# Exponentials of the decay sums loaded as rows, and several products, squares and loads moved, in a one-core decoder layer

## The chip, the cores and the metric

The kernel runs on one core of a Trainium2 chip. A core has five engines that run their own instruction streams side by side: PE (TensorE, matrix products), DVE (VectorE), ACT (ScalarE), POOL (GpSimd) and SP (SyncE), which here only issues loads; stores are issued by ACT. Data comes and goes through 16 DMA engines that all queues share. Each engine takes its instructions in order, and an instruction that waits holds up those behind it. The metric is device time in microseconds (us) from start to end of one execution.

## The reference

One layer of a decoder: the normed and modulated input h goes through one wide product into a gated spatial branch and a Mamba-2 branch, which are merged, projected and added to x.

```python
mod = silu(c) @ ada_w + ada_b                       # shift, scale, gate
h = rms_norm(x, norm_w) * (1 + scale) + shift       # x: 1024 x 1024
proj = h @ w_in                                     # 1024 x 11296
y_a = spatial_gating(gelu(gm_u), gelu(gm_v), ...) * silu(gm_z)
xbc = silu(causal_depthwise_conv(xbc, conv_w, conv_b)); xs, bm, cm = split(xbc)
dt = softplus(dt_raw + dt_bias); a = -exp(a_log)
y_b = ssd_scan(xs, dt, a, bm, cm) + xs * d_skip     # 8 groups, 32 heads of 64, state 128
y_b = rms_norm per group of (y_b * silu(ssm_z)), times ssm_norm_w
merged = sigmoid(g_a) * (y_a @ w_proj_a) + sigmoid(g_b) * (y_b @ w_proj_b)
out = rms_norm(x + gate * (merged @ w_out), final_norm_w)
```

The scan works in chunks of 128 rows. With A the running sum of dt * a inside a chunk, a chunk's output is

```python
y_diag = (C B^T * exp(A_l - A_s) for s <= l) @ (x dt)   # inside the chunk
y_off  = (C @ previous state) * exp(A_l)                # from the chunks before
state  = state * exp(A_end) + B^T @ (exp(A_end - A_s) * x dt)
```

The exp(A_l) of y_off, per head and row, is what the tile `ea` holds.

## The kernel before

**Stages.** In the profiled execution: up to 73 us the prologue (norm, modulation, the first gate product); to 149 us a block for the gated branch (V block); to 914 us the wide product as pairs of blocks with seven products in place of eight (`pair`, `jobs`), with convolutions, gates and the decay sums done beside it; to 1153 us the state-space stage; to 1340 us the product with `w_proj_b` (units p1, p3, p6, p5, p7, p2, p4 with eight parts each); then the output product. float32 operands are split into a high and a low part for the fast product format, so each product takes three matmuls (high x high, low x high, high x low).

**What sets the order.** Loads go through `load` (L90) on SP and keep the order of the program, as matmuls do (`mm` L81, `tp` L84). Stores go through `store` (L93) on ACT. `later(n, f)` puts a piece of work n slots on; a slot is one call of `run_tasks`. Other work on DVE, ACT and POOL is ordered by a scheduler, except where `pin` holds it in program order.

**Prologue.** For each of eight blocks, modulation rows (`pm`) are worked out and become `md` (DVE L275, L276), from which ACT and DVE form the operands of the gate product `acc`. SP loads `aw` and `w0r` for each block; between two of them the vectors `dtb`, `abc`, `dsk` (dt_bias, a_log, d_skip, each spread over 128 partitions). `small_parameters2` copies `dsk` into `dskt` on DVE (L503). The first product that uses `dskt` comes in the state-space stage.

**Decay sums.** `dt_part3`, about 745 us, holds A for 32 heads x 1024 rows in `act` and stores it as `acs_d`, one row of 4 heads x 256 per group and step.

**State-space stage.** 8 groups x 4 steps of 256 rows make 32 steps, two groups in turn. For each step n:
- `fetch` (SP): `dcy`, the row of `acs_d` spread over 128 partitions (512 KB), then `sl` (768 KB: C, B, x and silu(z) of the group). There are five sets of these tiles.
- `decay`: ACT takes the exponential of A for `ea` in two instructions of 64x512 (L1101), POOL masks `dcy` in place (L1104), ACT takes eight exponentials of it (L1109).
- `prep`: PE products `pc` and transposes `px`; DVE `xd`, `xe` (L1125), `dcy` times C B^T (L1129); ACT `bn` (L1131).
- `front`: PE `yi` and the state's product `sp`; the new state `st` on POOL (L1157) and DVE (L1159).
- `back`: PE `yn`; then `evacuate`: DVE `y` (L1185) and `ym` = yn * ea (L1189), POOL `y` + `ym` (L1190) and the gate product `yz` (L1191), which reads the last part of `sl` and so frees its buffer.
- after each second step `post`: two stores of `yz` to `yb_d` on ACT, then 5 slots on the squares (`squares`, in place in yz, ACT L1210 and POOL L1211), 17 slots on the row sums (`post2`: PE `pq`, DVE `ssq` L1221, POOL L1225). For the last half of the last two groups the squares go at once into other tiles (L1205, L1206), and the sums come after the loop.

`yz` has four buffers. Between these pieces, `draw` takes matmuls of the product with `w_proj_a` (`proj_a`, PE `pma`), 2 at a time, to fill PE. Its weights are cast to a high part (`wah`, ACT L1316) and a low part (`wal`, DVE L1317) one block of 128 columns ahead, after the second of eight products of the block before.

**Transition.** When the steps are done, all but five draws are taken, then `post2` of the last two groups, then `loads(u)` for the first six units of p1 (SP: `rb`, the row scales; `yn`, read from `yb_d`; `p1a`, `p1r`) with `operands` two units behind (DVE `yn` norm L1530; ACT `p1bh` L1567 and `p1a` L1572; their low parts on DVE), then the last draws, then `multiply` (L1592).

Of the kernel before, what the change touches and what calls it, by code (L numbers as in the profile page):

```python
# [8 lines left out]
F32 = mybir.dt.float32  # L9
# [26 lines left out]
def hybrid_kernel(  # L36
# [16 lines left out]
    def dt_(shape, name):  # L53
        return dram.tile(shape, F32, name=name, tag=name)

    acs_d = dt_([NG, 4, HPG, 256], "acs_d")
    rs_d = [dt_([1, S], f"rs_d{g}") for g in range(NG)]
    v_d = dt_([NG, P, NCH * P], "v_d")
    ya_d = [dt_([P, S], f"ya_d{g}") for g in range(NG)]
# [29 lines left out]
    def load(dst, src):  # L89
        pin(nc.sync.dma_start(dst, src))  # L90
# [77 lines left out]
    def wide(name, dt=F32):  # L168
        return w4[0].tile([P, S], dt, name=name, tag="w4", bufs=w4[1])


    with tc.tile_pool(name="p0", bufs=1, reuse_waits="tile") as p0:
# [278 lines left out]
        for n in range(1, KT):  # L451
            todo = prepare(n + 1) if n + 1 < KT else {}
            for at, _ in enumerate(first_products(n), 1):
                if at == 1 and n + 2 < KT:
                    load_aw(n + 2)
                    load_w0(n + 2)
                if at == 1 and n == 1:
                    load(dtb, dt_bias.to_broadcast([P, NH]))
                    load(abc, a_log.to_broadcast([P, NH]))
                    load(dsk, d_skip.to_broadcast([P, NH]))  # L460
                if at in todo:
                    todo[at]()
                if at == 2 and n < KT - 1:
                    split_w0(n + 1)
                between(n, at)
# [17 lines left out]

    def small_parameters():

        pkb = wide("pkb").rearrange("p (i q) -> p i q", q=P)
        G.memset(pkb[:, 0], 0.0)
        at = 0
        for src, n in [(conv_b, 32), (ssm_norm_w, 16), (gm_ln_w, 8), (gm_ln_b, 8)]:
            load(pkb[at : at + n, 0], src[0].rearrange("(r q) -> r q", q=P))  # L490
            at += n
        load(pkb[:, 1], conv_w[0].rearrange("k (i q) -> (k i) q", q=P))
        later(4, small_parameters2, pkb)
# [213 lines left out]
    def dt_part3():  # L707
        act = wide("act")[0:NH, :]
        for q in range(2):
            pt = bank(f"pact{q}")  # L710
            for i in range(4):
                ch = q * 4 + i
                tp(pt[0:NH, i * P : (i + 1) * P], nacs[:, ch * NH : (ch + 1) * NH], ident)
            V.tensor_scalar_mul(act[:, q * 512 : (q + 1) * 512], pt[0:NH, :], -1.0)
        for g in range(NG):
            store(acs_d[g].rearrange("s h t -> h s t"),
                  act[HPG * g : HPG * (g + 1), :].rearrange("h (s t) -> h s t", s=4))

    def mix_weights():

# [353 lines left out]
    class Group:  # L1074
# [5 lines left out]
        def fetch(self, s):  # L1080
            g, nm = self.g, f"{self.g}_{s}"
            n = nstep[0] % NSET
            nstep[0] += 1
            pool, b = (p2r, 2) if n < 2 else (p2q, NSET - 2)
            dcy = pool.tile([P, HPG, 2, P], F32, name=f"dcy{nm}", tag="dcy", bufs=b)
            load(dcy.rearrange("p h i l -> p (h i l)"),
                 acs_d[g, s].rearrange("h t -> (h t)").unsqueeze(0).to_broadcast([P, HPG * 256]))
            sl = pool.tile([P, 6, 256], F32, name=f"sl{nm}", tag="sl", bufs=b)
            load(sl, s_d[g][:, s])
            if n < 2:  # L1090
                ea = p2r.tile([P, 2, 256], F32, name=f"ea{nm}", tag="ea", bufs=2)
            else:
                ea = turn(ea_r, f"ea{nm}", F32).rearrange("p (j t) -> p j t", j=2)
            self.pre[s] = (sl, dcy, ea)

        def decay(self, s):

            g = self.g
            sl, dcy, ea = self.pre[s]
            for hh in range(2):  # L1100
                A.activation(ea[hh * HD : (hh + 1) * HD],  # L1101
                             dcy.rearrange("p (j e) i l -> p e j (i l)", e=2)[hh * HD : (hh + 1) * HD, hh], AF.Exp)
            d8 = dcy.rearrange("p h i l -> p (h i) l")
            G.affine_select(out=d8, in_=d8, compare_op=ALU.is_ge, fill=-1e30, base=0,  # L1104
                            pattern=[[0, 2 * HPG], [1, P]], channel_multiplier=-1)
            sub = fac(nacs, g, s)
            for i in range(2):
                for h in range(HPG):
                    A.activation(dcy[:, h, i, :], dcy[:, h, i, :], AF.Exp, bias=sub[:, i, h : h + 1])  # L1109
# [83 lines left out]
        def post(self, q):  # L1193

            g = self.g
            for j in range(2):
                store(yb_d[2 * g + j][:, q * 512 : (q + 1) * 512], self.yz[q][:, j])
            yz = self.yz[q]
            if g < NG - 2 or q == 0:
                later(5, self.squares, yz, [yz[:, j] for j in range(2)])  # L1200
                later(17, self.post2, q, [yz[:, 0]])
            else:
                self.late = sq = [turn(r, f"sq{g}", F32) for r in (ea_r, (ym_r, y1_r)[g % 2])]
                for j in range(2):
                    pin(A.activation(sq[j], yz[:, j], AF.Square))  # L1205
                G.tensor_add(sq[0], sq[0], sq[1])  # L1206

        def squares(self, yz, sq):
            for j in range(2):
# [102 lines left out]
    def wa_block(dd):  # L1312
        was[dd] = []
        for i, wr in enumerate(war.pop(dd)):
            wh, wl = turn(wah_r[0], f"wah{dd}_{i}"), turn(wal_r[0], f"wal{dd}_{i}")
            A.copy(wh, wr)  # L1316
            V.tensor_sub(wl, wr, f32(wh))  # L1317
            was[dd].append((wh, wl))

    def beside(n):  # L1320

        if n == 0:
            ya_load(0)
            ya_load(1)
        elif n == 1:
            for r, c in ((war_r, 2), (wah_r, 2), (wal_r, 2)):
                r.append(ring(c))
            wa_load(0)
            more = [room.pop(0) for _ in range(2)]
            room.extend(more)  # L1330
        elif n < 5:
            ya_load(2 * n - 2)
            ya_load(2 * n - 1)
        if n == 4:
            for k in range(2):
                ya_operand(k)
            wa_block(0)
            for k in range(2, 6):
                ya_operand(k)

# [56 lines left out]
    def proj_a():  # L1397

        for dd in range(KT):
            if dd + 2 < KT:  # L1400
                wa_load(dd + 2)
            ths, pms = [], []
            for h in range(2):
                th = turn(tha_r, f"tha{dd}_{h}", F32)
                load(th, th_d[dd * P : (dd + 1) * P, h * 512 : (h + 1) * 512])
                ths.append(th)
                pms.append(bank(f"pma{dd}_{h}"))
            for k in range(KT):
                wh, wl = was[dd][k // 4]
                yh, yl = yas[k]  # L1410
                ks = slice(k % 4 * P, (k % 4 + 1) * P)
                for n, (lw, r) in enumerate(((wh, yh), (wh, yl), (wl, yh))):
                    for h in range(2):
                        mm(pms[h], lw[:, ks], r[h], k + n == 0, k == KT - 1 and n == 2)
                    yield
                if k == 1 and dd + 1 < KT:
                    wa_block(dd + 1)
            keep = pin if dd == KT - 1 else lambda i: i
            for h in range(2):
                keep(V.scalar_tensor_tensor(ths[h], ths[h], 1.0, pms[h], op0=ALU.add, op1=ALU.mult))  # L1420
            for h in range(2):
                keep(nc.scalar.dma_start(mt_d[dd][:, h * 512 : (h + 1) * 512], ths[h]))
# [51 lines left out]
        run_tasks()  # L1474


    draw(left[0] - 5)
    for late in groups[NG - 2 :]:
        late.post2(1, late.late[:1])
    room.extend(ea_r[0] + [st_r[0][1]])  # L1480
    room.extend(tag for k in range(KT - 2) for tag in ya_tags[k])

# [200 lines left out]
    def ahead(u):  # L1683
        if u + LOAD < len(units):
            loads(u + LOAD)
        if u + LEAD < len(units):
            operands(u + LEAD)

    for u in range(LOAD):
        loads(u)  # L1690
        if u > 1:
            operands(u - 2)
    draw(left[0] + 1)
    room.extend(tag for k in (KT - 2, KT - 1) for tag in ya_tags[k])
    for tags, _ in (war_r[0], wah_r[0], wal_r[0], tha_r):
# [10 lines left out]
    for u, (nm, k) in enumerate(units):  # L1706
        if k == 0:
            if nm == "p1":
                first = {t: psb.tile([P, 512], F32, name=f"{t}p", tag=f"b{t}") for t in ('y0', 'y2', 'x0', 'x1', 'y1', 'x2', 'y3', 'x3')}
                psx, psy = ([first[f"{v}{j}"] for j in range(4)] for v in "xy")  # L1710
                rows_bank[0] = lambda name: psy[2 + ("pr6", "pr7").index(name)]
            elif nm in ("p5", "p2"):
                psy = banks(f"y{nm}", "y")
            ps = psy if nm in ("p2", "p5", "p3") else psx
# [216 lines left out]
```

## Time and profile before

| | us |
|---|---|
| median of three runs | 1400.12 |
| lowest, highest | 1399.70, 1400.92 |
| the profiled execution, its own time | 1404.41 |
| its span, first to last instruction | 1402.7 |
| mean granted PE clock of the profiled execution | 0.993 |

The profile is one execution. Times in it are counted from its first instruction. "Busy" is the time in which an engine executes; matmuls overlap each other a little, so the starts of matmuls, not their lengths, give their pace. A row of the timeline has start, length, engine, line, the tiles out<-in, and in brackets the idle time before it and what ended that. In the chain of waits each row is start, length, and what the end of the execution hung on at that moment. The granted clock is the share of full speed at which PE was let run.

### The profile page before, as it was taken

The page shows a single profiled execution, that of the slowest core. Times are in us where ns is not written, and L with a number is a line of the kernel's source. Part 1 is how long each engine was busy: PE and PEld are TensorE (multiplying, and loading weights), DVE is VectorE, ACT ScalarE, POOL GpSimd, SP SyncE. Part 2 cuts the span into 40 slices and gives each one's busy share as a digit, 9 for nine tenths or more (in the row PEclk, how much of TensorE's full clock was granted, in tenths as well). Part 3 has the DMA queues.
Part 4 walks back from the last instruction along what each step waited for, and adds up shares of the span by engine and source line. Part 5 has one row for each costly group of instructions (what it writes and reads, how often), then busy time and mean ns, then how long its engine had stood idle before and what let it go on. Part 6 is the DMA issues. An engine that isn't in the chain of part 4 may idle for free.

```text
span 1402.7 us, 20203 instructions
## 1 busy us (share of the span) xinstructions
PE 1370.8 (98%) x6951; PEld 1133.6 (81%) x6951; DVE 1041.7 (74%) x1724; ACT 800.0 (57%) x1447; POOL 189.1 (13%) x191
## 2 busy tenths in 40 slices
PE   8999999999999999999999999999999999999997
PEld 6588888888888888888888888888888877788786
DVE  4685876777778789788888885398777736859976
ACT  4664666667556566465576555677666714233443
POOL 1000000000000000000000000038868760000002
PEclk9999999999999999999999999999999999999999
DMA  8674534343435667787675764698787719978913
GB/s 265 176 234 137 151 120 121 100 126 118 130 99 148 195 196 246 229 260 210 196 218 177 234 205 139 212 362 305 270 272 266 266 65 323 346 250 298 381 63 120
DMA packets 247228, 288.60 MB, mean 206 GB/s; under 512 B 14509, under 2 KB 194133, under 8 KB 247125
## 3 DMA queue, kind: packets, MB, share of 16 engines
q1 hardware_dynamic: 173716, 203.76, 45.5%
q10 hardware_dynamic: 73408, 83.54, 17.5%
q8 instruction: 55, 0.90, 0.3%
q14 instruction: 49, 0.39, 0.1%
HBM read 199.79 MB, written 87.46 MB: 205 GB/s over the span
## 4 chain that ended last, share of the span: by engine, by line
PE 69%; DMA 11%; DVE 8%; ACT 4%; issue 3%; SPq 2%; POOL 2%; ACTq 0%; DVEq 0%; POOLq 0%
PE xz L565 6%; PE xx L565 6%; PE xg L565 5%; PE xcb L565 5%; PE xuz L565 5%; PE pma L81 3%; PE vx L954 3%; PE yx L565 3%; PE yz L565 3%; PE ycb L565 3%; PE yg L565 3%; PE ox L1775 2%; PE yuz L565 2%; SPq L90 2%; DMA yn<-yb_d 2%
## 5 line engine op out<-in xcount | busy, mean ns | idle before, releaser
L1104 POOL TENSOR_SCALAR_AFFINE_SELECT dcy<-dcy 128x1024 f32<-128x1024 f32 x32 | 35.0, 1092 | 794.6 <-DMA yl<-ya_d 748.6
L1109 ACT ACTIVATE dcy<-dcy,nacs 128x128 f32<-128x128 f32 x256 | 78.5, 388 | 14.1 <-POOL dcy L1104 13.7
L1101 ACT ACTIVATE ea<-dcy 64x512 f32<-64x512 f32 x64 | 40.1, 626 | 13.0 <-DMA dcy<-acs_d 12.5
L1189 DVE TENSOR_TENSOR ym<-yn,ea 128x512 f32<-128x512 f32 (+1 forms) x32 | 19.9, 622 | 32.8 <-PE yn L81 32.8
L81 PE MATMUL pma<-yh,wah 128*128 128x512 f32 x128 | 43.9, 424 | 0.0
L1129 DVE TENSOR_TENSOR dcy<-dcy,pc 128x1024 f32<-128x1024 f32 x32 | 38.9, 1217 | 5.0 <-PE pc L84 4.0
L81 PE MATMUL pma<-yh,wal 128*128 128x512 f32 x128 | 42.6, 414 | 0.0
L1024 ACT ACTIVATE ac<-ac 128x1024 f32<-128x1024 f32 x32 | 34.0, 1061 | 13.5 <-DVE ac L1022 13.2
L1191 POOL TENSOR_TENSOR yz<-y,sl 128x512 f32<-128x512 f32 x32 | 41.4, 1293 | 0.9
L81 PE MATMUL pma<-yl,wah 128*128 128x512 f32 x128 | 40.3, 396 | 0.0
L1530 DVE SCALAR_TENSOR_TENSOR yn<-yn,par,rb 128x512 f32<-128x512 f32 x32 | 23.8, 747 | 21.7 <-DMA yn<-yb_d 21.7
L1190 POOL TENSOR_TENSOR y<-y,ym 128x512 f32<-128x512 f32 (+1 forms) x32 | 36.5, 1142 | 14.6 <-DVE ym L1189 14.6
L81 PEld LDWEIGHTS yn<-sl,st 128*128 128x128 f32 x224 | 30.2, 191 | 8.4 <-POOL yz L1211 2.5
L81 PE MATMUL sp<-xe,bn 128*128 128x256 f32 x112 | 33.7, 418 | 3.1 <-DVE ssq L1221 1.6
L81 PE MATMUL yi<-dcy,xd 128*64 128x128 f32 x512 | 35.9, 284 | 0.7 <-DVE st L1159 0.7
L81 PE MATMUL yn<-sl,st 128*128 128x128 f32 x224 | 31.1, 276 | 5.2 <-DVE st L1159 5.2
L1790 POOL TENSOR_TENSOR r<-r,fnw 128x512 f32<-128x512 f32 x4 | 5.3, 1334 | 228.6 <-ACT junk L1788 228.6
L1022 DVE SCALAR_TENSOR_TENSOR ac<-c2x,cwt,ac 128x1023 f32<-128x1023 f32 (+2 forms) x24 | 30.7, 1280 | 6.2 <-ACT ac L1020 6.1
L1022 DVE SCALAR_TENSOR_TENSOR ac<-c2cb,cwt,ac 128x1023 f32<-128x1023 f32 (+2 forms) x24 | 30.6, 1275 | 5.6 <-ACT ac L1020 5.5
L824 ACT CAST wbb<-wbr 128x512 fp32r<-128x512 f32 x32 | 19.8, 619 | 26.1 <-DMA wb_d<-wbb 20.5
L986 ACT ACTIVATE vm<-vm,vr 128x128 f32<-128x128 f32 x64 | 25.8, 484 | 14.9 <-DMA vm<-v_d 10.3
L1157 POOL TENSOR_TENSOR st<-st,cd 128x256 f32<-128x256 f32 x48 | 32.9, 685 | 9.7 <-PE yn L81 6.3
(2974 smaller groups left out, 4385.3 us busy)
## 6 DMA issues: line engine op xcount, KB each, us to landing
sl<-s_d SPq DMA_DIRECT2D x32, 768.0 KB
s_d<-ac ACTq DMA_DIRECT2D x32, 512.0 KB
wb_d<-wbb ACTq DMA_DIRECT2D x32, 512.0 KB
dcy<-acs_d SPq DMA_DIRECT2D x32, 512.0 KB
av<-in_w_in_dram SPq DMA_DIRECT2D x36, 256.0 KB
aw<-in_ada_w_dram SPq DMA_DIRECT2D x16, 512.0 KB
wbr<-in_w_proj_b_dram SPq DMA_DIRECT2D x32, 256.0 KB
yb_d<-yz ACTq DMA_DIRECT2D x32, 256.0 KB
```

Of the source, the lines that this page charges most:

```text
L81: pin(PE.matmul(acc, l, r, start=first, stop=last))
L565: pin(PE.matmul(ps, lw[:, k * P : (k + 1) * P], r[k], start=first and n + k == 0, stop=n == 2 and k == 3, skip_group_check=not first))
L954: pin(PE.matmul(ps[pn][j], l[:, j * P : (j + 1) * P], r, start=nm in ("p1", "p5", "p2") and n + units[i][1] == 0, stop=n == 2 and k == 3, ...
L1022: V.scalar_tensor_tensor(ac[:, s:], cc[:, : S - s], conv_wt[:, 3 - s, i : i + 1], ac[:, s:], op0=ALU.mult, op1=ALU.add)
L1024: A.activation(ac, ac, AF.Silu)
L1101: A.activation(ea[hh * HD : (hh + 1) * HD], dcy.rearrange("p (j e) i l -> p e j (i l)", e=2)[hh * HD : (hh + 1) * HD, hh], AF.Exp)
L1104: G.affine_select(out=d8, in_=d8, compare_op=ALU.is_ge, fill=-1e30, base=0, pattern=[[0, 2 * HPG], [1, P]], channel_multiplier=-1)
L1109: A.activation(dcy[:, h, i, :], dcy[:, h, i, :], AF.Exp, bias=sub[:, i, h : h + 1])
L1129: V.tensor_tensor(d3, d3, pc[:, 0:256].unsqueeze(1).to_broadcast([P, HPG, 256]), op=ALU.mult)
L1157: G.tensor_mul(v3(s2), v3(self.st), fac(cd, g, s)[:, i].unsqueeze(2).to_broadcast([P, HPG, HD]))
L1190: G.tensor_add(y1[:, :, t0:], y1[:, :, t0:], m[:, :, t0:])
L1191: G.tensor_mul(yz, y1, sl[:, 4:6])
```

## The change

- `eas_d` is new in DRAM. `dt_part4`, two slots after the stores of A, takes one exponential of all of `act` on ACT; `dt_part5`, two slots on, stores it in 16 pieces: for each group and each parity of the head, rows of 2 heads x 256 per step.
- `fetch` issues two more loads per step on SP after `dcy` and `sl`: a row of 512 numbers spread over 64 partitions (128 KB), once for each half of `ea`. The two ACT instructions of L1101 are gone from `decay`.
- `dtb`, `abc` and `dsk` are loaded in `small_parameters`, behind the last load of the V block; the copies to `dskt` move along.
- `squares` and `post2` come three slots later for groups 0 to 5.
- The last two groups' second squares are taken in place in `yz`, five slots on, as the others.
- The low parts `wal` are formed after the fourth product of a block instead of the second.
- The transition: all but eight draws, `post2` of group 6, then the loads of four units, five more draws, `post2` of group 7, the other loads, the last draws. The order in which p1's PSUM tiles are given their banks is another.

```diff
@@ -54,6 +54,7 @@
         return dram.tile(shape, F32, name=name, tag=name)
 
     acs_d = dt_([NG, 4, HPG, 256], "acs_d")
+    eas_d = dt_([NG, 4, 2, HPG // 2, 256], "eas_d")
     rs_d = [dt_([1, S], f"rs_d{g}") for g in range(NG)]
     v_d = dt_([NG, P, NCH * P], "v_d")
     ya_d = [dt_([P, S], f"ya_d{g}") for g in range(NG)]
@@ -454,10 +455,6 @@
                 if at == 1 and n + 2 < KT:
                     load_aw(n + 2)
                     load_w0(n + 2)
-                if at == 1 and n == 1:
-                    load(dtb, dt_bias.to_broadcast([P, NH]))
-                    load(abc, a_log.to_broadcast([P, NH]))
-                    load(dsk, d_skip.to_broadcast([P, NH]))
                 if at in todo:
                     todo[at]()
                 if at == 2 and n < KT - 1:
@@ -483,6 +480,9 @@
 
     def small_parameters():
 
+        load(dtb, dt_bias.to_broadcast([P, NH]))
+        load(abc, a_log.to_broadcast([P, NH]))
+        load(dsk, d_skip.to_broadcast([P, NH]))
         pkb = wide("pkb").rearrange("p (i q) -> p i q", q=P)
         G.memset(pkb[:, 0], 0.0)
         at = 0
@@ -715,6 +715,17 @@
         for g in range(NG):
             store(acs_d[g].rearrange("s h t -> h s t"),
                   act[HPG * g : HPG * (g + 1), :].rearrange("h (s t) -> h s t", s=4))
+        later(2, dt_part4, act)
+
+    def dt_part4(act):
+        A.activation(act, act, AF.Exp)
+        later(2, dt_part5, act)
+
+    def dt_part5(act):
+        for g in range(NG):
+            for e in range(2):
+                store(eas_d[g, :, e].rearrange("s j t -> j s t"),
+                      act[HPG * g + e : HPG * (g + 1) : 2, :].rearrange("h (s t) -> h s t", s=4))
 
     def mix_weights():
 
@@ -1091,15 +1102,15 @@
                 ea = p2r.tile([P, 2, 256], F32, name=f"ea{nm}", tag="ea", bufs=2)
             else:
                 ea = turn(ea_r, f"ea{nm}", F32).rearrange("p (j t) -> p j t", j=2)
+            for hh in range(2):
+                load(ea[hh * HD : (hh + 1) * HD],
+                     eas_d[g, s, hh].rearrange("j t -> (j t)").unsqueeze(0).to_broadcast([HD, 512]))
             self.pre[s] = (sl, dcy, ea)
 
         def decay(self, s):
 
             g = self.g
             sl, dcy, ea = self.pre[s]
-            for hh in range(2):
-                A.activation(ea[hh * HD : (hh + 1) * HD],
-                             dcy.rearrange("p (j e) i l -> p e j (i l)", e=2)[hh * HD : (hh + 1) * HD, hh], AF.Exp)
             d8 = dcy.rearrange("p h i l -> p (h i) l")
             G.affine_select(out=d8, in_=d8, compare_op=ALU.is_ge, fill=-1e30, base=0,
                             pattern=[[0, 2 * HPG], [1, P]], channel_multiplier=-1)
@@ -1197,13 +1208,18 @@
                 store(yb_d[2 * g + j][:, q * 512 : (q + 1) * 512], self.yz[q][:, j])
             yz = self.yz[q]
             if g < NG - 2 or q == 0:
-                later(5, self.squares, yz, [yz[:, j] for j in range(2)])
-                later(17, self.post2, q, [yz[:, 0]])
+                late = 3 if g < NG - 2 else 0
+                later(5 + late, self.squares, yz, [yz[:, j] for j in range(2)])
+                later(17 + late, self.post2, q, [yz[:, 0]])
             else:
-                self.late = sq = [turn(r, f"sq{g}", F32) for r in (ea_r, (ym_r, y1_r)[g % 2])]
-                for j in range(2):
-                    pin(A.activation(sq[j], yz[:, j], AF.Square))
-                G.tensor_add(sq[0], sq[0], sq[1])
+                self.late = [yz[:, j] for j in range(2)]
+                later(5, self.late_squares)
+
+        def late_squares(self):
+            sq = self.late
+            for j in range(2):
+                pin(A.activation(sq[j], sq[j], AF.Square))
+            G.tensor_add(sq[0], sq[0], sq[1])
 
         def squares(self, yz, sq):
             for j in range(2):
@@ -1314,8 +1330,12 @@
         for i, wr in enumerate(war.pop(dd)):
             wh, wl = turn(wah_r[0], f"wah{dd}_{i}"), turn(wal_r[0], f"wal{dd}_{i}")
             A.copy(wh, wr)
+            was[dd].append((wh, wl, wr))
+
+    def wa_lows(dd):
+        for i, (wh, wl, wr) in enumerate(was[dd]):
             V.tensor_sub(wl, wr, f32(wh))
-            was[dd].append((wh, wl))
+            was[dd][i] = wh, wl
 
     def beside(n):
 
@@ -1335,6 +1355,7 @@
             for k in range(2):
                 ya_operand(k)
             wa_block(0)
+            wa_lows(0)
             for k in range(2, 6):
                 ya_operand(k)
 
@@ -1415,6 +1436,8 @@
                     yield
                 if k == 1 and dd + 1 < KT:
                     wa_block(dd + 1)
+                elif k == 3 and dd + 1 < KT:
+                    wa_lows(dd + 1)
             keep = pin if dd == KT - 1 else lambda i: i
             for h in range(2):
                 keep(V.scalar_tensor_tensor(ths[h], ths[h], 1.0, pms[h], op0=ALU.add, op1=ALU.mult))
@@ -1474,9 +1497,6 @@
         run_tasks()
 
 
-    draw(left[0] - 5)
-    for late in groups[NG - 2 :]:
-        late.post2(1, late.late[:1])
     room.extend(ea_r[0] + [st_r[0][1]])
     room.extend(tag for k in range(KT - 2) for tag in ya_tags[k])
 
@@ -1686,10 +1706,15 @@
         if u + LEAD < len(units):
             operands(u + LEAD)
 
+    draw(left[0] - 8)
+    groups[6].post2(1, groups[6].late[:1])
     for u in range(LOAD):
         loads(u)
         if u > 1:
             operands(u - 2)
+        if u == 3:
+            draw(left[0] - 3)
+            groups[7].post2(1, groups[7].late[:1])
     draw(left[0] + 1)
     room.extend(tag for k in (KT - 2, KT - 1) for tag in ya_tags[k])
     for tags, _ in (war_r[0], wah_r[0], wal_r[0], tha_r):
@@ -1706,7 +1731,7 @@
     for u, (nm, k) in enumerate(units):
         if k == 0:
             if nm == "p1":
-                first = {t: psb.tile([P, 512], F32, name=f"{t}p", tag=f"b{t}") for t in ('y0', 'y2', 'x0', 'x1', 'y1', 'x2', 'y3', 'x3')}
+                first = {t: psb.tile([P, 512], F32, name=f"{t}p", tag=f"b{t}") for t in ('y2', 'x0', 'x1', 'y0', 'x2', 'y1', 'x3', 'y3')}
                 psx, psy = ([first[f"{v}{j}"] for j in range(4)] for v in "xy")
                 rows_bank[0] = lambda name: psy[2 + ("pr6", "pr7").index(name)]
             elif nm in ("p5", "p2"):
```

## The prediction

> **What bounds the kernel now.** First the page's busy line, then busy time by stretch, cut where the change touches something.
>
> ```profile
> PE 1370.8 (98%) x6951; PEld 1133.6 (81%) x6951; DVE 1041.7 (74%) x1724; ACT 800.0 (57%) x1447; POOL 189.1 (13%) x191
> ```
>
> ```profile
> 30.00:46.00 16.00, 13.40 (x100) 8.43 (x94) 7.19 (x16) 7.76 (x14) 0.00 (x0) 0.89 0.68 193
> 149.00:914.00 765.00, 764.37 (x3441) 632.46 (x3441) 581.04 (x902) 470.18 (x739) 3.28 (x3) 1.00 0.56 174
> 750.00:775.00 25.00, 25.00 (x112) 20.69 (x111) 19.52 (x31) 17.02 (x27) 0.00 (x0) 1.00 0.75 233
> 905.00:1125.00 220.00, 210.44 (x1550) 182.40 (x1549) 165.74 (x297) 159.45 (x405) 156.08 (x152) 0.99 0.82 285
> 914.00:1153.00 239.00, 229.43 (x1678) 198.50 (x1677) 171.27 (x312) 153.15 (x391) 170.04 (x165) 0.99 0.74 259
> 1025.00:1045.00 20.00, 20.00 (x146) 17.50 (x145) 15.12 (x30) 13.91 (x37) 13.47 (x14) 0.91 0.79 252
> 1125.00:1145.00 20.00, 19.99 (x127) 16.77 (x126) 9.35 (x20) 1.52 (x3) 13.26 (x13) 0.94 0.15 54
> 1153.00:1340.00 187.00, 180.46 (x783) 146.85 (x783) 148.00 (x241) 67.13 (x117) 3.13 (x2) 0.98 0.89 315
> ```
>
> The columns are the window, its length, busy time of PE, PEld, DVE, ACT and POOL, then the granted PE clock, the DMA share and GB/s. PE is busy 1370.8 of 1402.7 us, and from 149 to 914 it never rests (764.37 of 765.00). The number of matmuls is not changed, so all that can be won is PE's 32 us of idle time and the stretches at less than full clock. What ended the idle time:
>
> ```profile
> PE yn L81 <- DVE st L1159: 5.2, 3, 2.4
> PE x0p L1592 <- ACT p1a L1572: 4.6, 1, 4.6
> PE pp L84 <- DMA pk<-in_ada_b_dram: 3.6, 1, 3.6
> PE acc L81 <- ACT b11h L300: 2.6, 1, 2.6
> PE sp L81 <- DVE ssq L1221: 1.6, 1, 1.6
> ```
>
> (Waiter, releaser, total us, times, longest.) Four of these five lie where the change works: one in the prologue (acc), two in the state-space stage (yn, sp), one at the step to the next product (x0p). The pp wait is the first load and stays. I take the four places in order of time.
>
> **Prologue: the three parameter loads leave SP's queue.** First the chain of waits, then DVE's and PE's timelines.
>
> ```profile
> 30.50 5.76 DMA dsk<-in_d_skip_dram
> ```
>
> ```profile
> 36.28 0.35 DVE L503 COPY dskt<-dsk 64x16 f32<-64x16 f32 x2 [4.35 <-DMA dsk<-in_d_skip_dram]
> 36.65 0.16 DVE L275 TENSOR_TENSOR md<-pm,par 128x1 f32<-128x1 f32 x1
> ```
>
> ```profile
> 32.14 0.50 PE L81 MATMUL pm<-ones,row 128*128 128x1 f32 x4
> ...
> 37.86 0.73 PE L81 MATMUL acc<-b11h,w0h 128*128 128x512 f32 x2 [2.60 <-ACT b11h L300]
> ```
>
> Two tiny copies of dsk stand in DVE's order ahead of md, and wait 4.35 us for a load issued at 30.50. The product that md reads was done at 32.64. With the copies gone md runs 4.0 us earlier (32.66 instead of 36.65), which is more than PE's pause of 2.60, so the pause goes whole. The clock column of 30 to 46 says 0.89: 0.11 x 16 = 1.8 us of full-clock work were lost, behind this pause and nowhere else in that window. Term: -2.6 - 1.7 = -4.3; bounds -2.6 (the clock drops anyway) and -4.4. The loads go behind the last weight load of the V block, about 107 us, where nothing stands behind them on SP until other small parameters; the copies cost DVE 0.35 us there, hidden unless DVE is late, at worst +0.35.
>
> [...]
>
> **Around 752 to 772 us: one exponential and 16 stores on ACT.** ACT's timeline, when the sums of the decays are stored:
>
> ```profile
> 748.59 1.28 ACT L1024 ACT_TABLE_LOAD   x1 [0.52 <-DMA acs_d<-act]
> 748.65 0.26 ACTq L93 DMA_DIRECT2D acs_d<-act  x1
> 749.88 1.06 ACT L1024 ACTIVATE ac<-ac 128x1024 f32<-128x1024 f32 x1
> ```
>
> New are one Exp over 32x1024 (as long as the 128x1024 row, 1.06), up to two table loads of 1.28, and 16 stores. A store held ACT's queue 0.26; say up to 0.4, 16 of them 4 to 6.5 us. In all 8 to 10 us of ACT. Between 750 and 775 ACT was idle for 25.00 - 17.02 = 8.0 us while PE was never idle, so it fits, spread over a little more than that window; the stores are due two slots after the Exp and run between ACT's evacuations. Term 0; if an evacuation of PSUM comes behind the Exp and both table loads without cover, +1.06 + 2 x 1.28 = +3.6, the other bound.
>
> **State-space stage: ea comes by DMA instead of by ACT.** The page's group, the wait that it causes, and a chain:
>
> ```profile
> L1101 ACT ACTIVATE ea<-dcy 64x512 f32<-64x512 f32 x64 | 40.1, 626 | 13.0 <-DMA dcy<-acs_d 12.5
> ```
>
> ```profile
> POOL dcy L1104 <- ACT ea L1101: 42.3, 19, 16.6
> ```
>
> ```profile
> 1004.53 7.82 DMA dcy<-acs_d
> ...
> 1016.08 3.89 DMA sl<-s_d
> ```
>
> Each of the 32 steps loses two ACT instructions of 626 ns, 1.25 us, between dcy's landing and the mask on POOL, and ACT no longer stands blocked until dcy has landed (12.5 us in all). Idle time here is 220 - 210.44 = 9.56 us, and the clock rows give 0.09 x 20 + 0.06 x 20 = 3.0 more: 12.6 us could be won. But not all of it hangs on ACT. The longest of the yn waits (2.4) ends the quoted chain: dcy lands after 7.82 us, ea, mask, the gate product on POOL that frees sl's buffer, then sl's own 3.89. For this chain the change gives 1.25 and takes something: two loads of 128 KB, each an issue of about 0.4 on SP (between 0.32 for a short load and 0.62, 2.47 / 4, for a long one, both quoted under the transition), stand between sl and the next step's dcy, and 256 KB at the stage's mean 285 GB/s are 0.9 us. dcy lands 1.7 us later, less 1.25, so this chain loses about 0.5. Other chains run through ACT and gain:
>
> ```profile
> 1073.10 0.63 ACT ea L1101
> ...
> 1073.76 0.63 ACT yz L1210
> ```
>
> ```profile
> 1117.30 0.63 ACT L1210 ACTIVATE yz<-yz 128x512 f32<-128x512 f32 x1 [1.04 <-DMA yb_d<-yz]
> 1117.36 1.29 ACTq L93 DMA_DIRECT2D yb_d<-yz  x2
> 1120.10 0.63 ACT L1210 ACTIVATE yz<-yz 128x512 f32<-128x512 f32 x1 [2.17 <-DMA yb_d<-yz]
> 1122.35 1.24 ACT L1210 ACTIVATE yz<-yz 128x512 f32<-128x512 f32 x2 [1.61 <-DMA yb_d<-yz]
> ```
>
> The first belongs to another of the yn waits (the three are 5.2, so 2.8 in the two shorter; I put 1.7 on this one): two ea and a square stood before the casts that DVE then waited for. The second is the sp wait of 1.6: squares of y wait in ACT's order for the store of the same tile to be read out, 1.04, 2.17, 1.61 us. Squares three slots later meet a finished store. I take 1.7 + 1.6 + the clock behind it 1.2 = 4.5, less 0.5 for the dcy chain: -4.0. The bounds are -12.6 and the first rival's +16. The squares' product moves with them, and a later gate product on POOL now must wait for it before it may overwrite the tile; POOL is idle 220 - 156.08 = 64 us in 28 steps, 2.3 a step, which hides it; behind such a wait POOL's y and the mask would queue. The low weight parts two products later are the same DVE work and are read one block later: 0.
>
> [...]
>
> **Transition: the first loads of the next product are issued before the last sums.** SP's, PE's and ACT's timelines and the chain:
>
> ```profile
> 1112.08 2.47 SPq L90 DMA_DIRECT2D tha<-th_d  x4
> 1152.67 0.32 SPq L90 DMA_DIRECT2D rb<-rs_d  x1
> ```
>
> ```profile
> 1154.53 5.83 DMA p1r<-in_w_proj_b_dram
> ```
>
> ```profile
> 1160.49 0.80 PE L1592 MATMUL x0p<-p1bh,p1a 128*128 128x512 f32 x1 [4.56 <-ACT p1a L1572]
> ...
> 1165.64 0.39 PE L1592 MATMUL x0p<-p1bh,p1a 128*128 128x512 f32 x1
> 1165.87 0.39 PE L1592 MATMUL x0p<-p1bl,p1a 128*128 128x512 f32 x1
> ```
>
> ```profile
> 1146.27 1.15 ACT L1205 ACTIVATE sq<-yz 128x512 f32<-128x512 f32 x2 [4.99 <-POOL yz L1191]
> ```
>
> SP stood still from 1114.55 (1112.08 + 2.47) to 1152.67, behind the last pq products; all of p1's loads came after that, and PE ran dry at 1160.49 - 4.56 = 1155.93. Its first 12 products then took 1165.64 - 1160.49 = 5.15 us at low clock where 12 x 0.23 = 2.76 is the later pace. So 4.56 + 2.39 = 7.0 us can go. In the changed order the first three units' loads no longer stand behind pq; they wait for a tile that step 29 of 0 to 31 frees, two steps of about 7 us (220 / 30) before the end, so about 1140, and take 6 us. What is late next: the last squares. They now work in place and must wait for their store; it is issued before 1146.27 and a store was read out 5 us after issue (1117.36 to 1122.35), so 1150.4, then 1.15 for squares and a POOL add of 128x512, 1.3 by the quoted pace of such tiles (twice ACT's 0.63): 1152.9. The last pq stands three draws (six matmuls at 0.23), about 1.4 us, before PE's end, 1154.5. That leaves 1.6 us, which p1's loads can use up by slowing the store. I take 1.5 us lost: term -5.5; bounds -7.0 and 0.
>
> **Sum.** -4.3 + 0 - 4.0 - 5.5 = -13.8 against the profiled execution's own 1404.4: 1390.6. That execution is 4.3 us above the median 1400.1 of the runs shown; carried to the median the forecast is 1386.3, so 1386.
>
> **The rivals.**
> 1. The ea loads make the state-space stage slower. Place: dcy on SP's queue, then the mask on POOL, in whose order the gate product that frees sl stands. For it: POOL waited through ACT for dcy 19 times, and dcy took 7.82 us where sl took 3.89, so the queue has bursts with no room; at that landing rate 256 KB would take 3.9 us. Against it: the DMA engines are idle 18% of the stage. Price: if dcy comes 2.0 us later, 0.75 x 19 = 14 more, and a half-clock stretch of 1.7: +16, with the two firm gains 1400.1 - 4.3 - 5.5 + 16 = 1406. It decides from (9.8 / 19 =) 0.5 us beyond 1.25, a dcy later by 1.8 us; my estimate is 1.7, so the margin rests on how many of the 19 waits reach PE. All of PE's idle time in the stage is 9.56 us against 42.3 that POOL waited so, a quarter, hence the small chance.
> 2. Only the prologue's gain stays: stalls in the stage move to other places, and the last squares stop PE as long as p1's operands did. 1400.1 - 4.3 = 1396.
> 3. The transition's gain is given back later: p1 to p4 run with the DMA share at 0.89 and 315 GB/s, so PE catches up with loads that come no sooner. 1386 + 5.5 = 1391.5. Against it: PE was busy 180.46 of 187 there, and 4.56 of the rest is the wait removed.
> 4. All idle time goes: -4.3 - 12.6 - 7.0 = -24, 1376.
>
> **How the numbers follow.** Forecast 0.50; rival 1 0.12; rival 2 0.13; rival 3 0.12; rival 4 0.13. The forecast's own spread is about 5 us each way. A range of 1377 to 1400 leaves out most of rival 1 and part of rival 4. What the runs can tell from no change is about 0.2%, 2.8 us: faster means under 1397.3. Forecast, rivals 3 and 4 are faster whole, rival 2 by two thirds: 0.83. Slower: most of rival 1, 0.11. The rest, 0.06, is the same.
>
> **What would show it.** In the changed trace: no acc wait on b11h and no dsk in the chain before 46 us, V block earlier by 4.3; PE still never idle around 752 to 775; POOL's mask waiting for dcy's DMA directly, dcy's landing 1 to 2 us longer, DMA share of the stage near 0.9, PE idle there about 6 us; SP issuing p1's loads before 1140 and x0p's wait under 2 us. Wrong would be: PE idle in the stage above 10 us with dcy or ea as the releaser, a wait of PE for pq's squares over 3 us at the end, or a PSUM wait near 760.

## The result and the profile after

The changed kernel takes 1387.43 us (median of four runs, 1386.12 to 1388.36) against 1400.52 for the kernel before in the same series: a ratio of 0.9904, 95% interval 0.9887 to 0.9922, or 13.4 us less (10.9 to 15.8). The forecast was 1386. The profiled execution took 1388.36 us, 16.0 less than that of before, which was a long one.

Busy time by stretch of the profile after, columns as before:

```profile
30.00:46.00 16.00, 15.98 (x122) 10.21 (x115) 9.79 (x21) 10.78 (x21) 0.00 (x0) 1.00 0.83 235
149.00:914.00 765.00, 764.34 (x3448) 633.35 (x3448) 583.25 (x901) 470.73 (x740) 3.63 (x3) 1.00 0.57 176
750.00:775.00 25.00, 25.00 (x112) 20.71 (x111) 18.84 (x31) 15.10 (x24) 0.00 (x0) 1.00 0.64 198
905.00:1125.00 220.00, 210.67 (x1560) 182.71 (x1560) 165.04 (x298) 115.74 (x328) 156.72 (x155) 0.99 0.95 315
914.00:1153.00 239.00, 229.04 (x1675) 197.94 (x1675) 172.92 (x316) 117.96 (x333) 170.56 (x164) 0.99 0.91 302
1153.00:1340.00 187.00, 187.00 (x827) 154.60 (x826) 152.75 (x250) 67.95 (x119) 2.01 (x1) 1.00 0.81 290
```

What ended PE's idle time, the longest:

```profile
PE yn L82 <- DVE st L1170: 7.3, 6, 2.8
PE pp L85 <- DMA pk<-in_ada_b_dram: 3.5, 1, 3.5
PE yi L82 <- DVE ym L1200: 1.4, 1, 1.4
```

The prologue's wait is gone and its clock is whole (1.00); the product with `w_proj_b` has no idle time left (187.00 of 187.00; from 1303 on this window holds the output product). In the state-space stage ACT lost 43.7 us of work (159.45 to 115.74) and the DMA share rose from 0.82 to 0.95, and PE is as idle as before: 9.33 us against 9.56. The `acc`, `x0p` and `sp` waits went; the `yn` waits grew from 5.2 to 7.3.

The starts of PE's first and last rows of each stage, read off its timeline, give the stages' lengths. "Wait" is from the last `pma` to the first `x0p` (0.23 where nothing is waited for, 0.43 for the same at low clock: in before p1's products start 0.43 apart from 1162.3 to 1164.5 at a clock of 0.50, and 0.23 apart from 1166 to 1168 at 1.00); "output" runs to the end of the span.

| kernel | V block starts | first yi to last pma | wait | x0p to first output product | output |
|---|---|---|---|---|---|
| before | 73.08 | 234.69 | 4.96 | 156.43 | 85.74 |
| before, second execution (b0) | 73.93 | 235.32 | 4.89 | 156.82 | 85.49 |
| after | 68.54 | 234.23 | 0.24 | 152.64 | 83.76 |
| e1 rows off | 68.13 | 231.20 | 0.23 | 159.20 | 83.69 |
| e8 rows off, banks fitted | 68.91 | 235.10 | 0.23 | 152.65 | 83.70 |
| e4 squares early | 68.15 | 235.24 | 6.49 | 154.88 | 83.68 |
| e9 squares early, banks fitted | 68.54 | 236.53 | 0.23 | 152.64 | 83.69 |
| e6 rows behind dcy | 68.49 | 235.40 | 0.24 | 152.64 | 84.23 |
| e3 old prologue | 71.94 | 232.12 | 0.23 | 152.63 | 83.72 |
| e2 old transition | 68.15 | 235.27 | 0.23 | 152.63 | 83.69 |
| e10b as e2, old late squares | 68.99 | 232.22 | 3.52 | 159.50 | 83.70 |
| b1 prologue alone | 68.11 | 233.98 | 5.11 | 155.83 | 83.70 |
| b2 in place alone | 73.69 | 236.27 | 0.43 | 153.13 | 83.73 |
| b3 both | 68.31 | 235.53 | 0.43 | 153.05 | 86.07 |

Of the 16.0 us between the two profiled executions, 4.5 come ahead of the V block, 0.6 up to the first yi, 0.5 from the stage, 8.5 from wait and product together, 2.0 from the output (there before's `oy` waited 1.36 us once; b0 and b3 show that wait too, b1 and b2, with the same code there, don't).

### The profile page after: what moved, and what is told of

Read it like the earlier page. It is cut to its first block, busy times and chain, and to the rows that moved or that the text cites. A ratio compares the mean times of both kernels' runs of the same rounds, so it can differ in the third digit from the quotient of the medians.

```text
span 1386.6 us, 20251 instructions
## 1 busy us (share of the span) xinstructions
PE 1364.4 (98%) x6951; PEld 1131.6 (82%) x6951; DVE 1041.4 (75%) x1724; ACT 764.3 (55%) x1386; POOL 190.0 (14%) x191
## 4 chain that ended last, share of the span: by engine, by line
PE 80%; DMA 7%; DVE 4%; POOL 3%; issue 2%; ACT 2%; SPq 1%; ACTq 0%; POOLq 0%; DVEq 0%
PE xcb L565 6%; PE xuz L565 6%; PE xx L565 6%; PE xz L565 5%; PE xg L565 5%; PE ox L1800 3%; PE vx L965 3%; PE yp L1612 3%; PE pma L82 3%; PE yuz L565 3%; PE ycb L565 3%; PE yz L565 3%; PE yx L565 3%; PE yg L565 2%; DMA ea<-eas_d 2%
## 5 line engine op out<-in xcount | busy, mean ns | idle before, releaser
L82 PEld LDWEIGHTS yi<-dcy,xd 128*64 128x64 f32 x512 | 27.8, 138 | 5.5 <-issue 2.2
```

Source lines behind the costliest of these rows:

```text
L82: pin(PE.matmul(acc, l, r, start=first, stop=last))
```

## The experiments

Times are given by the ratio to before, with its interval; 0.001 is 1.4 us. The changed kernel stands at 0.9904 (0.9887 to 0.9922). Some expectations name differences of medians instead, which are smaller for e1, e4 and e3: 5.0, 8.6 and 1.8 where the ratios give 6.7, 9.2 and 3.4.

### e1 and e8: the rows taken out

```diff
-            for hh in range(2):
-                load(ea[hh * HD : (hh + 1) * HD], eas_d[g, s, hh]...)
...
+            for hh in range(2):
+                A.activation(ea[...], dcy...[..., hh], AF.Exp)
...
-        later(2, dt_part4, act)
```

> The changed kernel, but ea is worked out on ACT from dcy again (64 exponentials, 40 us of ACT), without the 64 row loads and without the extra exponential and the 16 stores. Theory A, from the profile after, where the state-space stage's PE idle time is 9.3 us against 9.6 before and the DMA share 0.95 against 0.82: what ACT no longer does is paid back by dcy and sl landing later, so the rows are worth nothing: within 1.5 us of the changed kernel, and a DMA share near 0.82 in the stage. Theory B, the prediction's step: the rows are worth their share of the 4 us, and something else ate it: slower than the changed kernel by 3 or more, ACT in the chain of PE's waits. Theory C: the rows cost more than they bring, and without them it is faster by 2 or more.

e1: 0.9952 (0.9935 to 0.9968), 6.7 us slower than the changed kernel. But the table shows its state-space stage not longer, rather 3 us shorter; the loss is all behind x0p. The waits of PE in e1 and in e4 (next), one row each:

```profile
PE x1p L1611 <- DVE tha L1442: 4.7, 1, 4.7
```

```profile
PE x0p L1612 <- DVE tha L1443: 6.1, 1, 6.1
```

`tha` is the evacuation of the last `pma`. The chain of waits of e4 there:

```profile
1153.78 0.68 DVE p1a L1593
1154.46 1.21 DVE tha L1443 x2
1155.67 0.14 issue
1155.81 1.62 PE x0p L1612 x3
```

PE's products go to PSUM, used here as eight banks of one tile each that are handed round in a ring. `tha` stands in DVE's order behind a row of p1's operands, and the first product into the bank that `tha` empties waited for it, 4.7 us in e1 and 6.1 in e4. The allocations of the three programs say which: in the changed kernel the last two `pma` tiles lie in the banks of y0 and y1, needed only with p3; in e1 one lies in x1's, in e4 one in x0's. Without rows, or with squares earlier, the ring of banks stands elsewhere when p1 begins. e8 is e1 with the banks fitted:

```diff
-for t in ('y2', 'x0', 'x1', 'y0', 'x2', 'y1', 'x3', 'y3')
+for t in ('x0', 'y2', 'y0', 'x1', 'x2', 'y1', 'x3', 'y3')
```

> As e1 (ea on ACT again, no rows), with the banks of p1's accumulators given so that the last two pma banks and the last two pq banks go to y0 to y3, as in the changed kernel; in e1 the last pma bank but one had become x1's, and x1 waited 4.7 us for the tha that empties it. Theory A: e1's 5 us were that bank alone, and the rows are worth nothing or less: the state-space stage ends 3 to 4 us earlier than in the changed kernel and the whole is faster by 1 to 4. Theory B: the rows are worth something and the wait comes back elsewhere in the transition: slower than the changed kernel by 2 or more.

e8: 0.9907 (0.9890 to 0.9925), the changed kernel within 0.5 us. Busy time of the stretch 905 to 1125 in e8:

```profile
905.00:1125.00 220.00, 209.34 (x1559) 181.06 (x1559) 166.32 (x298) 153.54 (x393) 158.59 (x155) 1.00 0.81 280
```

ACT is back at 153.54 and the DMA share at 0.81, and PE is busy 209.34 against 210.67. The rows are worth nothing that these runs can tell. e1 and e8 have the same instructions in the same order on every engine, and up to x0p nothing differs; yet their stages took 231.20 and 235.10: that is how far this stage can differ from one execution to the next.

### e4 and e9: squares and row sums early

```diff
-                late = 3 if g < NG - 2 else 0
+                late = 0
```

> The changed kernel with squares 5 and row sums 17 slots on for all groups, as before. Theory A: with ACT freed by the rows, a square that waits for its store holds up nothing that PE needs soon, and the stage is bound by the loads: within 1.5 us. Theory B, the prediction's step: squares that wait 1 to 2 us for their store stop DVE and POOL and then PE, 1.6 us and 1.2 us of clock: slower by about 2.8.

e4: 0.9970 (0.9953 to 0.9986), 9.2 us slower; the wait of 6.1 at x0p is shown above. e9 has the banks fitted (`'y2', 'y1', 'x0', 'x1', 'x2', 'x3', 'y0', 'y3'`):

> As e4 (squares 5 and row sums 17 slots on for all groups), with the banks of p1's accumulators fitted in the same way; in e4 x0 had the last pma bank and waited 6.1 us for tha. Theory A: the wait and the low clock behind it, some 7 of e4's 8.6 us, were the bank: within 1.5 us of the changed kernel. Theory B: squares three slots earlier cost the stage 2.8 by themselves: slower by 2 to 3 still.

e9: 0.9915 (0.9901 to 0.9930), 1.5 us from the changed kernel, inside the intervals. The wait at x0p is gone, so it was the bank. Nothing shows that the three slots are worth anything.

### e6: rows behind the next dcy

```diff
+            for f in rows_due:
+                f()
+            rows_due.clear()
             sl = pool.tile(...)
             load(sl, s_d[g][:, s])
...
+            rows_due.append(lambda: [load(ea[...], eas_d[g, s, hh]...) for hh in range(2)])
```

> The changed kernel with each step's two row loads issued behind the next step's dcy instead of ahead of it; same bytes, same buffers. Theory A: the rows cost the stage through dcy, which they put back by about 1.7 us: the stage gets 2 to 3 us shorter, POOL waits less for dcy. Theory B: it is the bytes (DMA share 0.95) and not their order: within 1 us. Theory C: ea now comes last and DVE waits for it: slower by 2 or more.

e6: 0.9922 (0.9900 to 0.9943), 2.5 us slower by the ratio, the intervals overlap; the stage took 235.40. What POOL's mask waited for, first in e6, then in the changed kernel (total, times, longest; in both one wait of 24 to 26 us for the start of the stage):

```profile
POOL dcy L1121 <- DMA dcy<-acs_d: 50.9, 13, 26.2
```

```profile
POOL dcy L1115 <- DMA dcy<-acs_d: 27.7, 14, 6.4
POOL dcy L1115 <- DVE xd L1136: 23.9, 1, 23.9
```

50.9 - 26.2 = 24.7 in twelve against 27.7 in fourteen: hardly earlier. That the rows stand ahead of dcy is not what fills the stage.

### e2 and e10b: the transition

```diff
+    draw(left[0] - 5)
+    for late in groups[NG - 2 :]:
+        late.post2(1, late.late[:1])
     room.extend(ea_r[0] + [st_r[0][1]])
...
-    draw(left[0] - 8)
-    groups[6].post2(1, groups[6].late[:1])
     for u in range(LOAD):
         loads(u)
...
-        if u == 3:
-            draw(left[0] - 3)
-            groups[7].post2(1, groups[7].late[:1])
```

> The changed kernel with the old transition: all draws but five, the row sums of groups 6 and 7, then all loads of p1. The late squares stay in place in yz. Theory A: the loads behind the row sums were the whole of the wait, so it returns: 4.6 us wait at the first product of p1 and 2.4 of low clock, slower than the changed kernel by 7, up to 8.5 if the later units wait too. Theory B, the move of the squares into yz did part of it (SP's loads need no tile that the row sums read): 2 to 4 slower only.

e2: 0.9916 (0.9889 to 0.9943), 1.7 us from the changed kernel, its median 1385.64 the lowest of all. With the old order no wait at x0p comes back. What does come is a short wait for the last squares, and behind it the pace that before shows at low clock (0.86 and 0.94 from start to start of these pairs, where the changed kernel's stand 0.46 apart at a clock of 1.00 from 1144 to 1148):

```profile
1145.89 1.05 PE L82 MATMUL pq<-ones,yz 128*128 128x1 f32 x8 [0.68 <-POOL yz L1222]
1146.80 1.15 PE L82 MATMUL pma<-yl,wah 128*128 128x512 f32 x2
1147.74 1.05 PE L82 MATMUL pma<-yh,wal 128*128 128x512 f32 x2
```

The last `pma` pair starts at 1150.30, four pairs on: 3.50 - 4 x 0.46 = 1.7 us of clock and 0.68 of wait, 2.3 in this execution. The changed kernel has neither. So its order may be worth some 2 us, which the run times neither confirm nor exclude. SP's timeline in e2: p1's loads are written behind the last row sums and go out long before them, which PE did at 1144 to 1147.

```profile
1107.30 4.67 SPq L91 DMA_DIRECT2D tha<-th_d  x4
1112.07 1.12 SPq L91 DMA_DIRECT2D rb<-rs_d  x1
1122.94 0.32 SPq L91 DMA_DIRECT2D yn<-yb_d  x1
```

e10b takes out the squares in place as well:

```diff
-                self.late = [yz[:, j] for j in range(2)]
-                later(5, self.late_squares)
+                self.late = sq = [turn(r, f"sq{g}", F32) for r in (ea_r, (ym_r, y1_r)[g % 2])]
+                for j in range(2):
+                    pin(A.activation(sq[j], yz[:, j], AF.Square))
+                G.tensor_add(sq[0], sq[0], sq[1])
```

> As e2 (old transition), and the last two groups' second squares are taken at once into other tiles again (those of ea and ym or y1), as before. e2 alone was no slower than the changed kernel. Theory A: SP's first loads of p1 stood still because their tile was one of these, read by the last pq; with the squares in place no load has to wait for pq, and the order of loads and row sums is worth nothing: the wait of 4 to 5 us at x0p and the low clock return, slower than the changed kernel by 6 to 8. Theory B: the wait was of another origin (the run of before, the bank): within 2 us of e2.

e10b: 0.9974 (0.9961 to 0.9987), 9.8 us slower than the changed kernel and 8.1 slower than e2. SP's waits and timeline, and x0p, in e10b:

```profile
SPq L91 <- PE pq L82: 32.5, 1, 32.5
```

```profile
1108.63 4.55 SPq L91 DMA_DIRECT2D tha<-th_d  x4
1145.83 0.32 SPq L91 DMA_DIRECT2D rb<-rs_d  x1
```

```profile
1152.22 0.80 PE L1617 MATMUL x0p<-p1bh,p1a 128*128 128x512 f32 x1 [3.13 <-ACT p1a L1597]
```

This is the picture of before: SP stands still from 1113.2 to 1145.83. In the allocation of e10b and of before, the first load, `rb`, has the address of the tile that holds group 6's squares, which the last `pq` products still read. The PSUM banks of e10b are those of e2, so they don't differ here. It is the tile, and not the order, that brings the wait at x0p.

### e3 and b1: the prologue

```diff
+                if at == 1 and n == 1:
+                    load(dtb, ...); load(abc, ...); load(dsk, ...)
...
-        load(dtb, ...); load(abc, ...); load(dsk, ...)
```

> The changed kernel with the loads of dtb, abc and dsk back in the prologue between two weight loads; the copies to dskt follow their place in the order. Theory A: the wait of 2.6 us and the half clock behind it return, 4.3 to 4.6 slower than the changed kernel, and all stages behind it shift by that. Theory B: later stages take up a part (a load that comes in time anyway), 0 to 2 slower.

e3: 0.9928 (0.9906 to 0.9951), 3.4 us slower, though the intervals overlap a little. PE's wait of 2.8 us is back and the V block starts at 71.94, 3.4 later. The low clock that theory A expected did not come back: the clock of 30 to 46 is 1.00 in e3, where it was 0.89 in before.

```profile
PE acc L82 <- ACT b11h L301: 2.8, 1, 2.8
```

In its profiled execution the state-space stage, at 232.12, took most of that back, as it may by chance. b1 does the opposite, this part alone in the kernel before:

> The kernel before with the loads of dtb, abc and dsk moved behind the V block's last weight load, and nothing else. In e3 taking this part out of the changed kernel cost 1.8 us where the traces show the V block starting 3.4 later. Theory A: the prologue's 4.4 us are shortened in every run, but the state-space stage, whose length differs from run to run by some 4 us, blurs it: faster than before by 3 to 5, V block from 68.5. Theory B: later loads take back part of it always: faster by 1 to 2 only.

b1: 0.9971 (0.9958 to 0.9984), 4.1 us faster than before (2.2 to 5.9); the V block starts at 68.11, and the wait at x0p is still there (5.11). That is theory A.

### b2 and b3: in place alone, and the two together

b2 is the kernel before with the `late_squares` of the change; b3 has b1's edit too.

> The kernel before with the last two groups' second squares taken in place in yz, five slots on, and nothing else; loads, row sums and draws keep their order. Theory A: SP's wait of 38 us for pq goes with the tile, so x0p no longer waits: faster than before by 7 to 9. Theory B: in place is enough only together with the rows or the later squares (a free ACT): under 3 faster.

b2: 0.9943 (0.9922 to 0.9964), 8.0 us faster (5.0 to 10.9), and no wait at x0p.

> The kernel before with these two edits, and no other part of the change: no rows, no later squares, no other order of loads and draws, old banks. Theory A: the two are the whole gain: 12 to 14 us faster than before, within 1.5 us of the changed kernel. Theory B: the other parts carry a share: 3 or more slower than the changed kernel.

b3: 0.9919 (0.9896 to 0.9942), 11.3 us (8.1 to 14.6) against 13.4 for the whole change: the sum of the two, 12.1, within the intervals. Against the changed kernel it is 2.1 slower, between the two theories, and the intervals overlap. A small difference to the changed kernel can be seen in the clock from 1140 to 1160, first b3, then the changed kernel:

```profile
1140.00:1160.00 20.00, 19.70 (x93) 16.31 (x92) 16.12 (x26) 9.84 (x18) 6.65 (x4) 0.91 0.87 302
```

```profile
1140.00:1160.00 20.00, 20.00 (x102) 16.67 (x101) 15.01 (x26) 9.87 (x19) 6.85 (x4) 1.00 0.84 293
```

0.09 x 20 = 1.8 us, behind a wait of 0.3 for the last squares, just before the low clock; in the changed kernel the pq products stand apart and none waits. It is the same loss as in e2, and in both the last row sums stand in the old order.

### b0: the kernel before again

> The kernel before a second time, for how far its stages differ from one profiled execution to the next. Expected: prologue and transition as in the first (V block from 73.1, x0p's wait of 4 to 5 us); the state-space stage between 231 and 237 us, as over the kernels so far.

b0 took 1405.85 us: same waits at the same places (x0p 4.5, acc 3.2), stage 235.32. Over all series the kernel before ran between 1394.88 and 1406.14.

No version beat the changed kernel by more than the intervals.

## Why the prediction was right

The number was right, and so were two of its four terms. The other two were both off: the stage by 3.5 too much, the transition by 3.0 too little. That these two nearly cancel, and the sum comes within 1.4 us of the median, is luck.

**Prologue, -4.3.** Right in place and size: the V block starts 4.54 earlier, the clock of 30 to 46 is 1.00, and alone it is worth 4.1 (2.2 to 5.9). The share of the clock is no fixed price, though: with a pause of 2.60 in before the clock of 30 to 46 was 0.89, with 2.77 in b2 0.79, with 2.80 in e3 1.00.

**752 to 772, 0.** Right, with the price a little higher. ACT's timeline after:

```profile
747.38 1.28 ACT L721 ACT_TABLE_LOAD   x1
748.68 1.06 ACT L721 ACTIVATE act<-act 32x1024 f32<-32x1024 f32 x1
...
752.59 3.15 ACTq L94 DMA_DIRECT2D eas_d<-act  x3
755.78 0.62 ACT L551 CAST p4g10h<-a22g 128x512 fp32r<-128x512 f32 x1 [2.88 <-DMA eas_d<-act]
```

Exp and table load took what was said. A store of `eas_d` took 0.60 to 0.73 to issue, not 0.26 to 0.4, and the three of the row above filled 3.15 us. PE did not stop (25.00 of 25.00).

**State-space stage, -4.0.** Here a step failed, and not by its size alone. "1.7 + 1.6 + the clock behind it 1.2 = 4.5, less 0.5": each PE wait was put down to the ACT work that stood in its chain, as if PE would be free once that was gone. The `sp` wait did go, and others came (`yi` 1.4, `yn` 2.1 more), so PE was idle for 9.33 us where the prediction expected about 6. Nor did the later squares take the `sp` wait away for good: in e6, which has them, `sp` waits 1.6 for `ssq` again, and in e9, which has them early, it doesn't. With rows and without (e8), with squares early and late (e9), with the rows behind dcy (e6), the stage takes 234 to 237 us, where the same work took 231.2 and 235.1 in two executions. So neither ACT's 40 us nor the bytes decide it; the DMA engines went from 82 to 95% of their time without a loss that the runs can tell. What sets its 9 to 10 us of idle time (7 to 10 over all runs) stays open. In the changed kernel the chain of waits that ends in the longest `yn` wait (2.8, at 950.14) passes a row load of 7.84 us, so the rows may make a wait of their own in place of one they remove; that was not tested. The chain from 1083 to 1110 goes through POOL, which is busy 71 to 74% of the stretch in before, after, e1 and e8, but no run here changed POOL's work.

**Transition, -5.5.** The size was too small, as wait and product gave 8.5: the whole 7.0, a later wait of 0.6, and 0.9 that is not traced. Before's 187 us had 6.5 idle: 4.6 at the first x0p, and these two, of which the first lies in the output product (at 1331.81) and counts to its 2.0:

```profile
PE oy L1775 <- DVE wlt L1672: 1.4, 1, 1.4
PE x0p L1592 <- DVE p6bl L1568: 0.6, 1, 0.6
```

The loss of 1.5 to the last squares did not come: in the changed kernel no pq waits, and the first three units' operands were ready. With the old order of the row sums it did come, at 2.3 in e2 and 2.1 in b3. The step on the cause was wrong. The prediction let the loads come early because they "no longer stand behind pq"; e2 has them written behind it and has no wait at x0p, and e10b shows that the in-place squares, which the prediction named only as a risk, free the tile on which SP waited. In b2 they alone bring 8.0.

**Left out.** The new order of PSUM banks had no term. No run has the changed kernel with the old order; before and b3 have no such wait with theirs, so the new one seems only to keep that. With it unfitted the same edits cost 6 to 8 us (e1 against e8, e4 against e9). The output's 2.0 in the profiled execution had no term either; before, b0 and b3 have that wait and b1 and b2 have not, so it looks like chance. The later place of the low weight parts, a term of 0, was not tested alone.

**Rivals.** The first had its mechanism half: the mask now waits for dcy's landing itself (27.7 us in 14 waits, where before it waited 42.3 behind ea), at a DMA share of 0.95, but this did not reach PE. The second was right that the stage's waits move to other places, and wrong on the transition. The third falls with the 187.00 busy. The fourth was too hopeful on the stage.

## What to carry to other kernels

When a queue stands still, ask which buffer its next instruction will write and who still reads it, before the order of the program is changed: here a tile that was still read cost 8 us, and the order of loads and row sums was worth some 2 by the traces. A chain of waits through an engine tells what was last, not what PE gains when it is gone; where several chains are nearly as long, the next one can leave no gain at all. And where buffers go round in a ring, an edit upstream shifts who gets which: compare variants only with that fitted again.

## What was not expected of the hardware

Pauses of nearly the same length were not followed by the same clock. The pause before `acc` in the prologue was 2.77 us in b2 and 2.80 in e3, and the clock of 30 to 46 was 0.79 in b2 and 1.00 in e3:

```profile
30.00:46.00 16.00, 13.23 (x78) 8.55 (x78) 6.71 (x16) 6.49 (x12) 0.00 (x0) 0.79 0.67 187
```

```profile
30.00:46.00 16.00, 12.72 (x96) 8.17 (x93) 7.54 (x17) 8.18 (x15) 0.00 (x0) 1.00 0.66 184
```

In b3 a wait of 0.30 us amid thin pq products (one column each) was followed by low clock, 0.91 from 1140 to 1160, as the pace of the `pma` pairs shows (0.86 from start to start in place of 0.46):

```profile
1147.11 1.05 PE L81 MATMUL pq<-ones,yz 128*128 128x1 f32 x8 [0.30 <-POOL yz L1209]
...
1149.06 1.05 PE L81 MATMUL pma<-yh,wah 128*128 128x512 f32 x2
1149.92 1.05 PE L81 MATMUL pma<-yl,wah 128*128 128x512 f32 x2
```

In e8 a pause of 1.88 was followed by no low clock; that of the window about it is 1.00:

```profile
990.00 1.13 PE L82 MATMUL yn<-sl,st 128*128 128x128 f32 x8 [1.88 <-ACT bn L1141]
```

```profile
985.00:1005.00 20.00, 17.32 (x125) 14.58 (x122) 13.43 (x26) 14.30 (x41) 14.12 (x15) 1.00 0.70 214
```

Whether the thin products are the reason, or the moment at which a pause falls, no run here tested.
